# A decoder trunk on one core: the four convolution taps that TensorE took in three channel tiles go to VectorE

## The chip, the cores and the metric

One Trainium2 chip, one of its cores. The metric is device microseconds of one execution of the whole program, the median of several runs. TensorE is written PE, VectorE DVE, ScalarE ACT, GpSimd POOL and SyncE SP, as the profile writes them.

## The reference

Two layers over a sequence of 1024 positions and 1024 channels: forgetting attention and a gated convolutional feed-forward, then a Conformer convolution module and another feed-forward. The change lies in the Conformer module alone:

```
def conformer_conv(h, w_pw1, b_pw1, w_dw, b_dw, ln_g, w_pw2, b_pw2):
    u = h @ w_pw1 + b_pw1
    a, g = jnp.split(u, 2, axis=-1)
    u = a * jax.nn.sigmoid(g)
    u = causal_dwconv(u, w_dw) + b_dw
    u = rms_norm(u, ln_g)
    u = jax.nn.silu(u)
    return u @ w_pw2 + b_pw2
```

`causal_dwconv` is depthwise: each channel is convolved along the sequence with its own 31 taps (CONV_WIDTH = 31).

## The kernel before, in words

Channels lie on the 128 partitions and positions on the free axis. The sequence is taken in two halves of 512 positions; `conv(h)` (L1109) does half h, in eight channel tiles `ct` of 128 channels. fp32 products are made of three matmuls of split operands (`mm3`, L351, lines L354 to L356: high by high, low by high, high by low). A **piece** of such a product is 12 matmuls of 128x512; the weights of a piece are loaded (SP's queue), split into `whi` by ACT (L348, or L100 where the low part was stored earlier) and `wlo` by POOL or DVE (L349).

For each channel tile the module runs: four pieces of the pointwise product into two PSUM banks (`pw` in the trace); the gate (L1140), which is ACT's sigmoid `sg`, ACT's copy of 30 carried-over columns, and DVE's `u`, L1145; the taps (`taps_of`, L1169); and L1203, DVE's sum `y` of two accumulators. Of the 31 taps ten are made by ACT with POOL: ACT multiplies a shifted window (`prod`, L1195, the first one L1185) and POOL adds it to `pacc` (L1196). The others are DVE's: one instruction each, on the PSUM accumulator `cacc` (the first L1189, the next ones L1191). In the second half (`h == 1`) and the channel tiles of PE_TILES = (4, 5, 6) PE makes four of these (PE_TAPS): `on_pe` (L1159), put behind the gate, has ACT build four 128x128 diagonal matrices `dg` (L1166) and PE multiply them with the windows of `u` into `cacc` (L1167). DVE then adds its 17 taps to what PE left there.

The order of the instructions on the engines is written by hand: generators yield pieces, and `Trunk.trace` runs them with a look-ahead of a few splits. Each engine works its list in order. In the taps of a tile, `first` (L1219) mixes in other work: it counts DVE's tap instructions (`vector` of a piece) and lets a PE piece in for every BEAT = 3.6 of them, by turns from the next tile's `pw` pieces and from a `fill` generator. In the second half the fill is first the rest of the convolution's output product and its norm (transposes `nps`, L210, of the normed blocks `hn`, L201, turned into `hthi` and `htlo`, L322 and L323), then `early` (L509), the feed-forward's up-product pieces, `e` in the trace. Of these there is a fixed number in all: those not done in the taps are done later, two in the stretch in which `combine` (L447) has DVE form the factors `bhi`, `blo` of a Strassen-like product (L465 to L486), beside its first pieces `y` and `z`.

After the last tile the conv's norm follows: POOL adds the last square to `sqa` (L1217), PE sums it (`ssps`, L1253), POOL turns it into `r` (L171, L172), DVE makes a diagonal of it (L1261), PE spreads it (`rb`, L1265), DVE scales (L1271), ACT applies SiLU and casts (L1272, L1273), and the output product `dn` begins.

Of the kernel before, what the change touches and what calls it, by code (L numbers as in the profile page):

```python
# [9 lines left out]
F32 = mybir.dt.float32  # L10
F32R = mybir.dt.float32r
BF16 = mybir.dt.bfloat16
AF = mybir.ActivationFunctionType
# [4 lines left out]
P = 128  # L18
# [31 lines left out]

N_POOL = 10
ROW_BUFS = 8
PE_TAPS = 4
PE_TILES = (4, 5, 6)
GATES = (2, 1)
BEAT = (3.3, 3.6)
LAG = 3
# [57 lines left out]
class Trunk:  # L115
# [993 lines left out]
    def conv(self, xs, xd, h, ht, w_pw1, los, taps, vec, w_pw2, halo, after):  # L1109


        nc = self.nc
        C = taps.shape[1]
        H = C - 1
        n_pool = N_POOL
        wv = w_pw1.rearrange("(k p) n -> p k n", p=P)
        st = {}
        us = {}
        ys = {}
        accs = {}  # L1120

        def glu(ct):
            pss = [None, None]

            def piece(s, q):
                c0 = s * D + ct * P
                w = Weight(self, wv[:, 4 * q : 4 * q + 4, c0 : c0 + P], [P, 4, P], los[2 * ct + s][q])

                def run():
                    if q == 0:  # L1130
                        pss[s] = self.bank("pw1")
                    lh, ll = w.parts
                    hhi, hlo = ht[h]
                    for j in range(4):
                        k = 4 * q + j
                        self.mm3(pss[s], lh[:, j, :], ll[:, j, :], hhi.at(k), hlo.at(k), k == 0, k == KT - 1)

                return Piece(run, w.load, w.split, 1, tiles=1)

            def gate():  # L1140
                sg = self.part("sg")
                nc.scalar.activation(sg, pss[1], AF.Sigmoid, bias=vec[:, 1, ct : ct + 1])
                u = self.up_.tile([P, H + 512], F32, tag="u", name=self.n("u"), bufs=2)
                nc.scalar.copy(u[:, 0:H], halo[:, ct, :])
                nc.vector.scalar_tensor_tensor(  # L1145
                    u[:, H:], pss[0], vec[:, 0, ct : ct + 1], sg, op0=ALU.add, op1=ALU.mult
                )
                if h == 0:
                    nc.scalar.copy(halo[:, ct, :], u[:, 512:])
                us[ct] = u  # L1150

            for s in range(2):
                for q in range(2):
                    yield piece(s, q)
            yield Piece(gate, vector=1)
            if h == 1 and ct in PE_TILES:
                yield Piece(lambda: on_pe(ct))

        def on_pe(ct):  # L1159

            dg = self.part("dg")
            acc = accs[ct] = self.pst.tile([P, 512], F32, tag="t", name=self.n("cacc"))
            for i in range(PE_TAPS):
                j = n_pool + i
                d = dg[:, i * P : (i + 1) * P]
                nc.scalar.activation(d, self.ident, AF.Copy, scale=taps[:, j, ct : ct + 1])  # L1166
                nc.tensor.matmul(acc, d, us[ct][:, j : j + 512], start=i == 0, stop=i == PE_TAPS - 1)  # L1167

        def taps_of(ct):  # L1169
            begun = h == 1 and ct in PE_TILES  # L1170
            own = n_pool + (PE_TAPS if begun else 0)
            nv = C - own
            t = {}
            tap = lambda j: taps[:, j, ct : ct + 1]

            def some(i0, i1):
                if i0 == 0:
                    t["u"] = us.pop(ct)
                    t["acc"] = accs.pop(ct) if begun else self.pst.tile([P, 512], F32, tag="t", name=self.n("cacc"))
                    t["pacc"] = self.part("pacc")  # L1180
                    t["done"] = 0
                u, acc, pacc = t["u"], t["acc"], t["pacc"]
                win = lambda j: u[:, j : j + 512]
                if i0 == 0:
                    nc.scalar.activation(pacc, win(0), AF.Identity, bias=vec[:, 2, ct : ct + 1], scale=tap(0))  # L1185
                for i in range(i0, i1):
                    j = own + i
                    if i == 0 and not begun:
                        nc.vector.tensor_scalar(acc, win(j), tap(j), None, op0=ALU.mult)  # L1189
                    else:  # L1190
                        nc.vector.scalar_tensor_tensor(acc, win(j), tap(j), acc, op0=ALU.mult, op1=ALU.add)  # L1191
                    while t["done"] < min(n_pool - 1, (n_pool - 1) * (i + 1) // (nv - 2)):
                        t["done"] += 1
                        p = self.part("prod")
                        nc.scalar.activation(p, win(t["done"]), AF.Copy, scale=tap(t["done"]))  # L1195
                        nc.gpsimd.tensor_tensor(pacc, pacc, p, op=ALU.add)  # L1196

            def end():
                if ct == 0:
                    st["yq"] = [self.quarter("y", F32, late=True) for _ in range(2)]  # L1200
                    st["sqa"] = self.part("sqa")
                y = ys[ct] = st["yq"][ct // 4][:, ct % 4, :]
                nc.vector.tensor_tensor(y, t["acc"], t["pacc"], op=ALU.add)  # L1203

            for i in range(0, nv, 3):
                yield Piece(lambda i=i: some(i, min(i + 3, nv)), vector=min(3, nv - i))
                if i == 6 and ct > 0:
                    yield Piece(lambda: square(ct - 1))
            yield Piece(end, vector=1)

        def square(ct):
            if ct == 0:
                nc.scalar.activation(st["sqa"], ys[ct], AF.Square)
            else:
                sq = self.part("sq")
                nc.scalar.activation(sq, ys[ct], AF.Square)
                nc.gpsimd.tensor_tensor(st["sqa"], st["sqa"], sq, op=ALU.add)  # L1217

        def first(fill):  # L1219

            beat = turn = 0
            yield from glu(0)
            for ct in range(KT):
                gates = glu(ct + 1) if ct + 1 < KT else iter(())
                for t in taps_of(ct):
                    while beat > 0:

                        own = turn < GATES[h]
                        p = None
                        for g in ([gates] + fill)[:: 1 if own else -1]:  # L1230
                            if not p:
                                p = next(g, None)
                                own = g is gates
                        if not p:
                            beat = 0
                            break
                        turn = (turn + 1) % (GATES[h] + 1) if p.tiles else GATES[h] if own else 0
                        yield p
                        beat += p.vector - (BEAT[h] if p.tiles else 0)
                    yield t  # L1240
                    beat += t.vector
                for p in gates:
                    turn = GATES[h]
                    yield p
            yield Piece(lambda: square(KT - 1))
# [68 lines left out]
def trunk(ctx, tc, a):  # L1314
# [205 lines left out]
    def pieces():  # L1520
# [10 lines left out]
        down1 = ffn_down(0, 1, xds[0], conv_norm, dnlo, actlo)  # L1531
        yield from turned(down1)
        main0, norm0, rest0 = conv(0)
        yield from main0([down1])
        yield from some(down1, 3)
# [5 lines left out]
        yield from down1  # L1541
        yield from turned(rest0)
        main1, norm1, rest1 = conv(1)
        fill = [rest0]
        main1 = main1(fill)
# [59 lines left out]
```

## Time and profile before

| | |
|---|---|
| median of 3 runs | 2355.17 us (2353.74 to 2355.51) |
| the profiled execution, own time | 2358.65 us |
| its span | 2356.9 us |
| PE busy | 2270.7 us, 96% of the span |
| DVE busy | 1648.0 us, 70% |
| ACT busy | 1359.7 us, 58% |
| POOL busy | 1402.2 us, 59% |

The span runs from the first to the last instruction; the 1.75 us between it and the execution's own time lie around it. Busy time of PE comes from modelled ends of pipelined matmuls: a matmul is listed with 0.39 us, yet the next one starts 0.23 us behind it, so lengths of PE work are read from starts. The stretch that the change touches runs from about 1538 us (the gate of tile 3 in the second half) to about 1697 us (the first `dn` of the output product).

### The profile page before, as it was taken

The numbers are of one execution on the slowest core, as the hardware profiler recorded it, in microseconds if no ns is written. First come the engines' busy times: TensorE is split into PE (matmuls) and PEld (weight loads), VectorE is DVE, ScalarE is ACT, GpSimd is POOL, SyncE is SP. The second block draws the span as 40 slices with busy tenths as digits, with TensorE's granted clock in tenths as the row PEclk, the third lists the DMA queues.
The fourth block names the chain that finished last, engine by engine and source line by source line (L and its number), as shares of the span: only waits on it lengthen the run. The fifth ranks groups of instructions, "written<-read, shape, count | busy, mean of one in ns | idle before, by whom it ended". The sixth has DMA issues, their size and how long they took to land.

```text
span 2356.9 us, 35332 instructions
## 1 busy us (share of the span) xinstructions
PE 2270.7 (96%) x11306; PEld 1934.8 (82%) x11306; DVE 1648.0 (70%) x2740; ACT 1359.7 (58%) x2844; POOL 1402.2 (59%) x1187
## 2 busy tenths in 40 slices
PE   7899999999999999999999999978999999999998
PEld 7899999997878887778778887856787888888887
DVE  5577777777378999997337985885738999993222
ACT  5566666666255666666455665555635666664443
POOL 3445545444018988884454895765634999965543
PEclk9999999998999999999999999999999999999999
DMA  4222322143155556666888777533555545466664
GB/s 144 64 79 79 81 77 77 57 166 131 69 176 184 155 161 213 200 198 200 285 273 291 235 251 264 176 110 112 183 180 170 155 152 156 153 220 208 216 206 155
DMA packets 366842, 392.64 MB, mean 167 GB/s; under 512 B 26416, under 2 KB 245312, under 8 KB 366656
## 3 DMA queue, kind: packets, MB, share of 16 engines
q1 hardware_dynamic: 366656, 390.38, 52.1%
q8 instruction: 89, 1.46, 0.2%
q14 instruction: 97, 0.79, 0.1%
HBM read 299.78 MB, written 82.12 MB: 162 GB/s over the span
## 4 chain that ended last, share of the span: by engine, by line
PE 44%; DVE 18%; issue 5%; ACT 3%; DMA 2%; POOL 2%; SPq 0%; DVEq 0%; ACTq 0%; POOLq 0%
DVE acc L580 9%; PE dn L355 7%; PE dn L356 7%; PE dn L354 7%; PE pw L354 2%; PE pw L356 2%; PE pw L355 2%; DVE cacc L1191 2%; PE e L356 1%; PE e L354 1%; PE e L355 1%; ACT acc L584 1%; PE y L354 1%; PE y L355 1%; PE y L356 1%
## 5 line engine op out<-in xcount | busy, mean ns | idle before, releaser
L349 POOL TENSOR_TENSOR wlo<-raw,whi 128x512 fp32r<-128x512 f32 (+1 forms) x305 | 443.0, 1454 | 270.1 <-ACT whi L348 237.2
L348 ACT CAST whi<-raw 128x512 fp32r<-128x512 f32 (+2 forms) x497 | 302.7, 633 | 248.3 <-PE dn L355 159.2
L349 DVE TENSOR_TENSOR wlo<-raw,whi 128x512 fp32r<-128x512 f32 (+1 forms) x192 | 149.5, 783 | 236.8 <-ACT whi L348 221.3
L349 POOL TENSOR_TENSOR wlo<-s,whi 128x512 fp32r<-128x512 f32 x176 | 258.7, 1480 | 66.8 <-ACT whi L348 66.6
L354 PE MATMUL dn<-whi,whi 128*128 128x512 f32 x704 | 276.1, 392 | 1.8 <-ACT whi L348 1.3
L355 PE MATMUL dn<-wlo,whi 128*128 128x512 f32 x704 | 275.2, 391 | 0.9 <-POOL wlo L349 0.9
L356 PE MATMUL dn<-whi,wlo 128*128 128x512 f32 x704 | 275.3, 391 | 0.0
L1191 DVE SCALAR_TENSOR_TENSOR cacc<-u,ctaps,cacc 128x512 f32<-128x512 f32 x311 | 235.0, 756 | 21.9 <-PE cacc L1167 11.5
L1196 POOL TENSOR_TENSOR pacc<-pacc,prod 128x512 f32<-128x512 f32 x144 | 190.1, 1320 | 87.2 <-ACT prod L1195 80.7
L354 PE MATMUL y<-bhi,whi 128*128 128x512 f32 x528 | 207.2, 392 | 6.6 <-DVE u L638 5.2
L356 PE MATMUL y<-bhi,wlo 128*128 128x512 f32 x528 | 205.6, 389 | 0.0
L355 PE MATMUL y<-blo,whi 128*128 128x512 f32 x528 | 205.5, 389 | 0.0
L171 POOL TENSOR_SCALAR ss<-ss 128x4 f32<-128x4 f32 (+1 forms) x96 | 22.8, 238 | 298.5 <-ACT hn L191 156.3
L354 PE MATMUL pj<-whi,hthi 128*128 128x384 f32 (+1 forms) x512 | 178.1, 349 | 5.3 <-DVE zf L824 3.6
L356 PE MATMUL pj<-whi,htlo 128*128 128x384 f32 (+1 forms) x512 | 177.5, 347 | 0.0
L355 PE MATMUL pj<-wlo,hthi 128*128 128x384 f32 (+1 forms) x512 | 176.5, 345 | 0.7 <-DVE wlo L349 0.7
L914 POOL TENSOR_SCALAR x<-x,nm 128x896 f32<-128x896 f32 (+7 forms) x128 | 101.0, 794 | 107.0 <-DVE nm L913 75.3
L558 POOL TENSOR_TENSOR s<-raw,raw 128x512 f32<-128x512 f32 x88 | 124.6, 1416 | 63.7 <-DMA raw<-in_ffn_w_up_dram 35.7
L354 PEld LDWEIGHTS dn<-whi,whi 128*128 128x128 f32 x704 | 132.9, 189 | 30.3 <-ACT whi L348 1.7
L355 PEld LDWEIGHTS dn<-wlo,whi 128*128 128x128 f32 x704 | 132.9, 189 | 29.1 <-POOL wlo L349 1.2
L356 PEld LDWEIGHTS dn<-whi,wlo 128*128 128x128 f32 x704 | 132.9, 189 | 27.6
L584 ACT ACTIVATE acc<-acc 128x512 f32<-128x512 f32 x88 | 55.7, 633 | 166.2 <-DVE acc L580 164.9
(224 smaller groups left out, 6442.8 us busy)
## 6 DMA issues: line engine op xcount, KB each, us to landing
raw<-in_ffn_w_up_dram SPq DMA_DIRECT2D x240, 256.0 KB
raw<-in_ffn_w_down_dram SPq DMA_DIRECT2D x176, 256.0 KB
raw<-actd SPq DMA_DIRECT2D x152, 256.0 KB
raw<-in_conv_w_pw_dram SPq DMA_DIRECT2D x96, 256.0 KB
actd<-acc SPq DMA_DIRECT2D x76, 256.0 KB
wlo<-pwlo SPq DMA_DIRECT2D x64, 256.0 KB
raw<-in_fox_w_in_dram SPq DMA_DIRECT2D x64, 192.0 KB
xd<-x SPq DMA_DIRECT2D x24, 512.0 KB
```

What stands on the lines that cost most here:

```text
L171: nc.gpsimd.tensor_scalar(ss, ss, 1.0 / n, EPS, op0=ALU.mult, op1=ALU.add)
L348: self.nc.scalar.copy(hi, raw)
L349: (self.nc.vector if vector else self.nc.gpsimd).tensor_tensor(lo, raw, f32(hi), op=ALU.subtract)
L354: nc.tensor.matmul(out, lh, rh, start=start, stop=False, skip_group_check=more)
L355: nc.tensor.matmul(out, lh, rl, start=False, stop=False, skip_group_check=more)
L356: nc.tensor.matmul(out, ll, rh, start=False, stop=stop, skip_group_check=more)
L558: nc.gpsimd.tensor_tensor(st[o], *(st[m].rearrange("p a b -> p (a b)") if m[0] == "a" else st[m] for m in ((y, x) if o == "s4" else (x, y) ...
L580: nc.vector.scalar_tensor_tensor(acc[:, j:], ps[:, : 512 - j], tap[2 - j], acc[:, j:], op0=ALU.mult, op1=ALU.add)
L584: nc.scalar.activation(acc, acc, AF.Silu)
L914: nc.gpsimd.tensor_scalar(X[:, :L], X[:, :L], nm[:, 2:3], 1.0, op0=ALU.mult, op1=ALU.mult)
L1191: nc.vector.scalar_tensor_tensor(acc, win(j), tap(j), acc, op0=ALU.mult, op1=ALU.add)
L1196: nc.gpsimd.tensor_tensor(pacc, pacc, p, op=ALU.add)
```

## The change

PE_TAPS, PE_TILES, `on_pe` and the branches on `begun` go. Every tile of both halves has 21 taps on DVE (one L1189, twenty L1191) and ten on ACT with POOL.

```
-PE_TAPS = 4
-PE_TILES = (4, 5, 6)
...
             yield Piece(gate, vector=1)
-            if h == 1 and ct in PE_TILES:
-                yield Piece(lambda: on_pe(ct))
-
-        def on_pe(ct):
-
-            dg = self.part("dg")
-            acc = accs[ct] = self.pst.tile([P, 512], F32, tag="t", name=self.n("cacc"))
-            for i in range(PE_TAPS):
-                j = n_pool + i
-                d = dg[:, i * P : (i + 1) * P]
-                nc.scalar.activation(d, self.ident, AF.Copy, scale=taps[:, j, ct : ct + 1])
-                nc.tensor.matmul(acc, d, us[ct][:, j : j + 512], start=i == 0, stop=i == PE_TAPS - 1)
 
         def taps_of(ct):
-            begun = h == 1 and ct in PE_TILES
-            own = n_pool + (PE_TAPS if begun else 0)
-            nv = C - own
+            nv = C - n_pool
...
-                    t["acc"] = accs.pop(ct) if begun else self.pst.tile([P, 512], F32, tag="t", name=self.n("cacc"))
+                    t["acc"] = self.pst.tile([P, 512], F32, tag="t", name=self.n("cacc"))
...
                 for i in range(i0, i1):
-                    j = own + i
-                    if i == 0 and not begun:
+                    j = n_pool + i
+                    if i == 0:
                         nc.vector.tensor_scalar(acc, win(j), tap(j), None, op0=ALU.mult)
                     else:
                         nc.vector.scalar_tensor_tensor(acc, win(j), tap(j), acc, op0=ALU.mult, op1=ALU.add)
```

Up to the gate of tile 4 in the second half, each engine's list stays as it was. From there it moves, because the taps that `first` counts are more. Line numbers below are each kernel's own: L1191, L201, L210, L323, L349, L354 of before are L1174, L199, L208, L321, L347, L352 now.

PE, behind the last `pw` piece of tile 4; `cacc` is the taps' accumulator, `nps` the transposes of the normed blocks, `pw` the products of tile 5. Before:

```order
L356 MATMUL pw_3619_17569<-hthi_3415_16562,wlo_17433 128x512
L1167 MATMUL cacc_17635<-u_17631,dg_17634 128x512 x4
L210 MATMUL nps_17644<-ident,hn_17556 128x128 x4
L210 MATMUL nps_17651<-ident,hn_17556 128x128 x4
L210 MATMUL nps_17673<-ident,hn_17625 128x128 x4
L210 MATMUL nps_17680<-ident,hn_17625 128x128 x4
L354 MATMUL pw_3643_17694<-hthi_3414_16561,whi_17456 128x512
```

With the change:

```order
L354 MATMUL pw_3619_17569<-hthi_3415_16562,wlo_17433 128x512
L208 MATMUL nps_17640<-ident,hn_17556 128x128 x4
L208 MATMUL nps_17647<-ident,hn_17556 128x128 x4
L352 MATMUL pw_3638_17663<-hthi_3414_16561,whi_17456 128x512
L353 MATMUL pw_3638_17663<-htlo_3416_16563,whi_17456 128x512
```

The tap products ahead of the transposes are gone, and a `pw` piece now stands between the first and the second block's transposes. Further on, the third and the fourth block's transposes stand side by side, where a `pw` piece lay between them.

DVE at the same place, from the gate of tile 4 (`u_17631`) to its sixth tap or so; `cacc_17486` is tile 3's accumulator. Before:

```order
L1145 SCALAR_TENSOR_TENSOR u_17631<-pw_3605_17503,cvec,sg_17629 128x512
L323 TENSOR_TENSOR htlo_3603_17498<-nps_17644,hthi_3601_17496 128x4x128
L323 TENSOR_TENSOR htlo_3604_17499<-nps_17651,hthi_3602_17497 128x4x128
L201 SCALAR_TENSOR_TENSOR hn_17625<-x_16629,ss_17624,rows_16833 128x512
L201 SCALAR_TENSOR_TENSOR hn_17625<-x_16629,ss_17624,rows_16835 128x512
L1191 SCALAR_TENSOR_TENSOR cacc_17486<-u_17483,ctaps,cacc_17486 128x512 x3
L1203 TENSOR_TENSOR y_17085<-cacc_17486,pacc_17487 128x512
```

With the change:

```order
L1142 SCALAR_TENSOR_TENSOR u_17631<-pw_3605_17503,cvec,sg_17629 128x512
L1174 SCALAR_TENSOR_TENSOR cacc_17486<-u_17483,ctaps,cacc_17486 128x512 x3
L321 TENSOR_TENSOR htlo_3603_17498<-nps_17640,hthi_3601_17496 128x4x128
L321 TENSOR_TENSOR htlo_3604_17499<-nps_17647,hthi_3602_17497 128x4x128
L199 SCALAR_TENSOR_TENSOR hn_17625<-x_16629,ss_17624,rows_16833 128x512
L199 SCALAR_TENSOR_TENSOR hn_17625<-x_16629,ss_17624,rows_16835 128x512
L1186 TENSOR_TENSOR y_17085<-cacc_17486,pacc_17487 128x512
```

Tile 3's last three taps moved ahead of the `htlo` that waits for PE's transposes.

DVE in the stretch of `combine`, where the last factor `blo` is made; `wlo` is the split of an `e` piece's weight, `t` and `blo` the factors. Before:

```order
L476 TENSOR_TENSOR t_3996_19376<-t_3996_19376,htlo_3604_17499 128x512
L349 TENSOR_TENSOR wlo_19574<-raw_19361,whi_19573 128x512
L486 TENSOR_TENSOR blo_19554<-t_3980_19335,bhi_19553 128x512
L475 TENSOR_TENSOR t_4003_19412<-hthi_3602_17497,t_4003_19412 128x512
L476 TENSOR_TENSOR t_4003_19412<-t_4003_19412,htlo_3604_17499 128x512
L349 TENSOR_TENSOR wlo_19598<-raw_19401,whi_19597 128x512
L628 TENSOR_TENSOR u_4040_19614<-y_19601,p_3827_18577 128x512
```

With the change:

```order
L474 TENSOR_TENSOR t_4001_19402<-t_4001_19402,htlo_3604_17499 128x512
L484 TENSOR_TENSOR blo_19578<-t_3986_19363,bhi_19577 128x512
L473 TENSOR_TENSOR t_4007_19436<-hthi_3602_17497,t_4007_19436 128x512
L474 TENSOR_TENSOR t_4007_19436<-t_4007_19436,htlo_3604_17499 128x512
L626 TENSOR_TENSOR u_4051_19654<-y_19641,p_3833_18605 128x512
```

Two weight splits have gone from here: on PE, the two `e` pieces that stood among the first `y` and `z` pieces are done earlier. Of them one comes ahead of `ssps` and one between `rb` and the first `dn`.

## Rows read from the trace of the kernel before

**Rows 1.** The page's part 1: busy time and share of each engine.

```profile
PE 2270.7 (96%) x11306; PEld 1934.8 (82%) x11306; DVE 1648.0 (70%) x2740; ACT 1359.7 (58%) x2844; POOL 1402.2 (59%) x1187
```

**Rows 2.** Busy time by stretch: start:end, length, then each engine, PEclk, DMA.

```profile
1538.00:1558.00 20.00, 11.69 (x51) 8.98 (x49) 18.32 (x27) 13.16 (x26) 15.68 (x15) 0.95 0.24 73
1558.00:1600.00 42.00, 27.92 (x105) 18.47 (x106) 30.36 (x39) 19.11 (x36) 18.83 (x17) 0.87 0.31 110
1650.00:1674.00 24.00, 24.00 (x107) 19.88 (x107) 23.47 (x32) 14.43 (x25) 17.01 (x12) 1.00 0.56 176
```

**Rows 3.** Who waited for whom on PE, 1550 to 1698 us: total, times, longest.

```profile
PE cacc L1167 <- DVE u L1145: 16.5, 3, 8.2
PE nps L210 <- DVE hn L201: 7.6, 5, 2.2
```

**Rows 4.** PE's timeline: start, length, instruction, idle time before it and releaser.

```profile
1550.14 0.39 PE L356 MATMUL pw<-hthi,wlo 128*128 128x512 f32 x1
1558.77 5.61 PE L1167 MATMUL cacc<-u,dg 128*128 128x512 f32 x8 [8.24 <-DVE u L1145]
1564.22 1.03 PE L210 MATMUL nps<-ident,hn 128*128 128x128 f32 x8
...
1596.08 5.73 PE L1167 MATMUL cacc<-u,dg 128*128 128x512 f32 x8 [5.71 <-DVE u L1145]
...
1623.51 5.37 PE L1167 MATMUL cacc<-u,dg 128*128 128x512 f32 x8 [2.60 <-DVE u L1145]
...
1689.55 1.02 PE L1265 MATMUL rb<-dg,ones 128*128 128x512 f32 x2
1697.14 0.50 PE L354 MATMUL dn<-whi,hthi 128*128 128x512 f32 x1 [1.11 <-ACT hthi L1273]
```

**Rows 5.** Who waited for whom on DVE, 1558 to 1674.2 us.

```profile
DVE cacc L1191 <- PE cacc L1167: 11.5, 2, 5.9
DVE htlo L323 <- ACT hthi L322: 6.8, 1, 6.8
DVE wlo L349 <- ACT whi L348: 5.7, 2, 3.4
DVE y L1203 <- POOL pacc L1196: 5.4, 2, 3.9
```

**Rows 6.** DVE's timeline: a run of 16 taps, hn and gate of tile 4, y of tiles 4 and 7.

```profile
1524.86 12.63 DVE L1191 SCALAR_TENSOR_TENSOR cacc<-u,ctaps,cacc 128x512 f32<-128x512 f32 x16
1556.54 1.43 DVE L201 SCALAR_TENSOR_TENSOR hn<-x,ss,rows 128x512 f32<-128x512 f32 x2
1557.88 0.74 DVE L1145 SCALAR_TENSOR_TENSOR u<-pw,cvec,sg 128x512 f32<-128x512 f32 x1
1594.59 0.69 DVE L1203 TENSOR_TENSOR y<-cacc,pacc 128x512 f32<-128x512 f32 x1
1673.45 0.69 DVE L1203 TENSOR_TENSOR y<-cacc,pacc 128x512 f32<-128x512 f32 x1
```

**Rows 7.** PE's granted clock (behind the busy times) in pieces of 2 us.

```profile
1556.00:1558.00 2.00, 0.00 (x0) 0.00 (x0) 2.00 (x4) 0.00 (x0) 1.83 (x3) 0.50 0.62 198
1564.00:1566.00 2.00, 1.25 (x9) 0.79 (x7) 0.53 (x1) 1.15 (x3) 0.00 (x0) 1.00 0.00 0
```

**Rows 8.** The norm's chain behind the last tile: POOL's and DVE's timelines.

```profile
1674.88 1.29 POOL L1217 TENSOR_TENSOR sqa<-sqa,sq 128x512 f32<-128x512 f32 x1 [5.88 <-ACT sq L1216]
1687.23 1.89 DVE L1261 TENSOR_SCALAR dg<-ident,r 128x128 f32<-128x128 f32 x4 [5.11 <-POOL r L172]
```

**Rows 9.** The stretch of combine: PE's first and seventh piece, DVE's last blo.

```profile
1800.35 0.39 PE L354 MATMUL y<-bhi,whi 128*128 128x512 f32 x1
...
1816.67 0.39 PE L354 MATMUL y<-bhi,whi 128*128 128x512 f32 x1
...
1815.48 0.84 DVE L486 TENSOR_TENSOR blo<-t,bhi 128x512 fp32r<-128x512 f32 x1
```

**Rows 10.** The page's part 5: POOL's adds of ACT's taps, mean of one.

```profile
L1196 POOL TENSOR_TENSOR pacc<-pacc,prod 128x512 f32<-128x512 f32 x144 | 190.1, 1320 | 87.2 <-ACT prod L1195 80.7
```

More of the change, by code (lines that the diff above doesn't have):

```diff
@@ L1119, in conv @@
         ys = {}
-        accs = {}
         def glu(ct):
```

## The prediction

> **What bounds the kernel now.** Read first the busy times: PE has work for 96% of the span and DVE for 70% [rows 1], so over the whole program time is PE's, and a change shows only where PE stands still or works less. Then the stretches: from 1538 to 1600 us that picture is turned round, PE is busy in 11.69 of 20 us and in 27.92 of 42, while DVE has 18.32 of 20 and 30.36 of 42 [rows 2]. This is the stretch in which the taps run. The waits say why it is loose on both sides. PE waits 16.5 us in front of its tap products for DVE's `u`, three times, and 7.6 us in front of transposes for `hn` [rows 3]. DVE in turn waits 11.5 us for those tap products, and 6.8 us for `hthi` [rows 5], whose transposes stand right behind the first tap product on PE: that product begins at 1558.77 and the transposes at 1564.22 [rows 4]. So once per tile 4, 5 and 6, the two engines stop for one another: PE can't begin the taps before the gate's `u`, and DVE can't go on before PE has ended them. The tap products are slow as well: PE's granted clock is 0.50 of its 2.4 GHz in 1556 to 1558 and back at 1.00 only in 1564 to 1566 [rows 7], so the first tap product runs wholly at 1.2 GHz or on its way back.
>
> **The change, on DVE.** Each of the three tiles gets four more taps (17 become one L1189 and twenty L1191): 12 more in all. A tap follows the last one by 12.63 / 16 = 0.79 us [rows 6], so 9.5 us more work. From the end of tile 4's gate (1557.88 + 0.74 = 1558.6) to the end of tile 7's `y` (1673.45 + 0.69 = 1674.1) [rows 6] there are 115.5 us. DVE waits 11.5 + 6.8 + 5.7 + 5.4 = 29.4 us in them [rows 5], so it works 86.1 us; with the new taps 95.6 us. If no wait is left, `y` of tile 7 comes 19.9 us earlier. The 11.5 go with the tap products. The 6.8 go because the transposes are no longer behind them and three taps of tile 3 now stand between. The 5.7 for `whi` and the 5.4 for POOL's `pacc` stand late because ACT sat behind an `e` piece that sat behind the tap products. POOL's own work for a tile is nine adds of 1.32 us [rows 10], and a square of 1.29 us [rows 8]; with two weight splits taken at that same length it is 15.8 us, below DVE's 21 x 0.79 + gate 0.74 + `y` 0.69 = 18.0 us per tile, so POOL keeps up. I leave 2 us of waits: 17.9 us earlier. Bounds: 19.9 if none is left, 8.8 if all 11.1 us of waits on `whi` and `pacc` stay.
>
> ACT loses the twelve diagonals, which nobody waits for once the products are gone; SP's list is the same up to a few swapped neighbours. Both go at nothing: ACT is busy 19.11 of 42 us there [rows 2].
>
> **The change, on PE.** From the end of the last `pw` in front of the stall (1550.14 and the 0.23 us to where a next one would start, 1550.4) to the first `dn` at 1697.14 there are 146.8 us. Taken off it: idle 16.5 + 7.6 [rows 3] + 1.1 [rows 4] = 25.2 us, and the three tap products. These are listed with 5.61, 5.73 and 5.37 us; the first one's follower starts 5.45 us behind it [rows 4], so about 16 us together. The rest, 105.6 us, stays. Two `e` pieces come in: seven pieces' starts, 1800.35 to 1816.67, are six pieces apart, 2.72 us each [rows 9], so 5.4 us and 111.0 us of work.
>
> New idle time: the first transposes still wait for DVE's `hn`, done at 1556.54 + 1.43 = 1558.0 [rows 6]: 7.6 us. The second block's wait is covered by the `pw` piece that moved in front of it, but the third's and fourth's now have none between: DVE does three taps, a split, `htlo` and `hn` between them, some 6 us. I take the old 7.6 us again for all of these. That gap sends the clock down as the one before it did [rows 7]; the first gap's slow work ends in a wait anyway, the second one's slows the `pw` pieces of tile 5, for which I take half of four microseconds, 2 us. In front of `rb` I take 2.5 us (next paragraph). Together 19.7, so `dn` begins at 1550.4 + 130.7 = 1681.1, **16.1 us earlier**.
>
> DVE must bear that out. POOL's last square ended at 1674.88 + 1.29 = 1676.2 and `rb` began at 1689.55 [rows 8, 4], 13.4 us for the chain through `ssps`, `r` and `dg`; 17.9 us earlier it is 1658.3, and `rb` at 1671.7 if the chain is as long, some 4 us earlier if part of it was `ssps` standing behind `e` pieces. From `rb` to `dn` were 7.6 us [rows 4]; now three `e` pieces, 8.2 us, and `rb`'s own 1.0 stand there: 9.2. That gives 1677 to 1681. PE has three pieces, 8.2 us, between `ssps` and `rb`, so it comes up some 2.5 us short: that is the wait I put in. PE's sum is the later one, and decides.
>
> In the stretch of `combine` the two `e` pieces are missing: **5.4 us less**, provided that nothing they covered comes out. The first piece on the last factor began one piece behind 1816.67, at 1819.4, and would now begin at 1814.0; its last quarter, 2.0 us on, needs the last `blo`, which ended at 1815.48 + 0.84 = 1816.3 [rows 9]. Two weight splits leave DVE in front of it; at the 0.84 us of `blo` that is 1814.6 against 1816.0. It just fits.
>
> Sum: 16.1 + 5.4 = 21.5 us off the profiled execution's 2358.65, so 2337.2. The median of the runs, 2355.17, lies 3.5 us below that execution; the same 21.5 off it is **2333.7 us**. With DVE's bounds, `dn` comes 7.0 to 20.6 us earlier, and the time is 2342.8 to 2329.2.
>
> A rule that speaks against the change: in the stretch 1558 to 1600 the busiest engine is DVE, not PE [rows 2], and it is given 9.5 us more. The Trainium skill, Perfetto Trace Analysis, section Identifying the Most-Contended Engine, says that the engine with the highest occupancy is the one to relieve first. By that rule DVE's stretch would grow by the whole 9.5 us. The rows of waits decide for me: an engine that waits 29.4 us has room for 9.5. The case in which it has none is the rival "no change" below.
>
> **The rivals.** What a measurement of this kernel can tell from no change is about 0.2%, 4.7 us.
>
> *More than that.* PE runs through: of its idle time only the first 7.6 us stay, and it gains 16 + 25.2 - 7.6 = 33.6 us, time 2321.6. For it: from 1650 to 1674 PE is never idle [rows 2]. Against it: there DVE is busy 23.47 of 24 us, so DVE would have to lose more than it can (19.9).
>
> *Less.* The moved pieces were cover: without them PE waits for `blo` and the weights of `y` in `combine` and loses the 5.4 us again, and the norm's chain in front of `rb` costs 5 us more. 21.5 - 10.4 = 11.1, time 2344.1. For it: the margin at `blo` is 1.4 us.
>
> *No change.* DVE's waits keep their length under other names (`pacc`, `whi`), so the tiles grow by the 9.5 us, less the 5.4 us of the moved pieces: 2359.3. It decides where POOL's chain takes as long as a tile did, (1673.45 - 1594.59) / 3 = 26.3 us [rows 6], against my 15.8.
>
> *Slower.* PE's clock: the products that bridged part of the gaps are gone, and bursts of `pw` and `e` between the longer gaps run at 1.2 GHz. A piece costs 2.72 us more at 0.50; from eight such pieces on the 21.5 us are eaten, and at ten the time is 2355.2 + 27.2 - 21.5 = 2360.9. Against it: before, the clock was back some 5 to 7 us behind the restart [rows 7, 4], about two pieces per gap, and I see two gaps that long. The Trainium skill, TensorE: Matmul & The Clock Gate, section HAM oscillation, tells of a kernel in which every burst starts at half clock behind every gap; the row bears out the drop, not that it would repeat.
>
> That the change does not do what it says can be left out: the engines' lists show the products gone and the taps there.
>
> **How the numbers follow.** Forecast 0.70, more 0.08, less 0.11, no change 0.06, slower 0.05. The forecast's own range is 2329 to 2343; going down to 2323, towards "more", and up to 2345, over "less", leaves out the last two and part of "more". Faster by over 0.2%: 0.70 + 0.08 + 0.11 = 0.89; within 0.06; slower 0.05.
>
> **What would show it.** In the new profile: no L1167; 320 taps of the later form (311 before) and 16 first ones (13); DVE with few waits from 1558 us, and its last `y` ending near 1656; POOL's `pacc` not among DVE's long waits; `dn` beginning near 1681, PE idle some 20 us in front of it; no wait of a `y` or `z` piece in the stretch of `combine`. I am wrong if `y` of tile 7 ends later than 1665 (waits stayed), if the granted clock is below 1.00 for more than the two gaps, or if PE waits in `combine`.

## The result, and the profile with the change

| | median, us | runs | ratio to before, 95% interval |
|---|---|---|---|
| before, beside the change | 2355.28 | 4 (2353.74 to 2355.51) | |
| with the change | 2339.14 | 4 (2335.43 to 2341.47) | 0.9931 [0.9914, 0.9949] |
| with the change, once more in a later job | 2338.32 | 4 (2334.36 to 2339.73) | 0.9920 [0.9906, 0.9935] |

The change makes the kernel faster by 16.1 us in the first comparison and by 18.6 us in the second (before: 2356.93 us there). The forecast was 21.5 us less, 2333.7 us; the range of 2323 to 2345 holds both medians. The profiled execution took 2338.83 us, its span 2337.1.

The page's parts 1 and 5 of the changed kernel, and the first taps from the view of lines; they answer to [rows 1]:

```profile
PE 2259.7 (97%) x11282; PEld 1930.9 (83%) x11282; DVE 1653.6 (71%) x2751; ACT 1354.6 (58%) x2832; POOL 1405.7 (60%) x1188
...
L1174 DVE SCALAR_TENSOR_TENSOR cacc<-u,ctaps,cacc 128x512 f32<-128x512 f32 x320 | 241.7, 755 | 10.8
...
L1172 DVE TENSOR_SCALAR cacc<-u,ctaps 128x512 f32<-128x512 f32 x16 | 12.0, 749 | 0.8
```

PE lost its 24 tap matmuls; DVE has 320 later taps and 16 first ones, as the lists say. The stretches that were loose in [rows 2], in the same order of columns (start:end, length, PE, PEld, DVE, ACT, POOL, clock, DMA):

```profile
1538.00:1558.00 20.00, 13.17 (x55) 10.81 (x54) 19.39 (x28) 13.20 (x25) 17.37 (x17) 0.86 0.35 118
1558.00:1600.00 42.00, 37.11 (x159) 29.96 (x159) 39.03 (x53) 25.79 (x47) 26.76 (x23) 0.91 0.46 146
...
1650.00:1674.00 24.00, 20.00 (x80) 15.51 (x79) 11.07 (x17) 8.86 (x17) 11.78 (x10) 0.88 0.61 198
```

From 1558 to 1600 both engines are now nearly full, where they stood at 27.92 and 30.36 us of 42. The last row covers later work than it did [rows 2]: the norm's chain, which before began at 1674.88 us [rows 8], now lies in it. It shows new trouble: PE has 4 us of idle time there and a clock of 0.88. Who waited, on PE from 1548 to 1685 us, answering to [rows 3]:

```profile
PE nps L208 <- DVE hn L199: 11.7, 4, 6.8
PE rb L1248 <- DVE dg L1244: 4.0, 1, 4.0
```

and on DVE from 1556 to 1651.8 us, the end of the last `y`, answering to [rows 5]:

```profile
DVE u L1142 <- ACT sg L1139: 0.9, 1, 0.9
DVE wlo L347 <- ACT whi L346: 0.8, 1, 0.8
DVE htlo L321 <- ACT hthi L320: 0.2, 1, 0.2
```

DVE's 29.4 us of waits have become 1.9, the 2 us that the forecast left, and `pacc` is not among them. Another 2.6 us of waits for `whi` lie behind the last `y`; the expectations below count them in (4.6 us).

**A point to measure from.** The two traces differ before the place that the change touches. DVE's gate of tile 3 stands in both kernels behind the same list of instructions, and yet it starts 3.16 us sooner with the change. DVE's timeline, before:

```profile
1539.30 0.75 DVE L1145 SCALAR_TENSOR_TENSOR u<-pw,cvec,sg 128x512 f32<-128x512 f32 x1 [1.00 <-ACT sg L1142]
```

and with the change, with the last `y`:

```profile
1536.14 0.75 DVE L1142 SCALAR_TENSOR_TENSOR u<-pw,cvec,sg 128x512 f32<-128x512 f32 x1 [1.00 <-ACT sg L1139]
...
1651.04 0.68 DVE L1186 TENSOR_TENSOR y<-cacc,pacc 128x512 f32<-128x512 f32 x1
```

One variant that was profiled twice (four pieces and filled gaps, below) has this gate at 1538.88 and at 1532.97 us, but 796.8 and 796.5 us from the gate to the end of the span. So all places below are counted from this gate, the third gate of the expectations:

| us behind the gate of tile 3 | end of last `y` | `rb` begins | first `dn` | end of span |
|---|---|---|---|---|
| before | 134.8 | 150.3 | 157.8 | 817.6 |
| with the change | 115.6 | 132.8 | 144.9 | 801.0 |
| with the change, once more | 115.2 | 132.4 | 144.3 | 800.5 |
| tap products in tile 4 alone | 119.2 | 135.2 | 144.5 | 805.1 |
| tap products in tiles 5 and 6 alone | 125.9 | 140.8 | 148.6 | 806.3 |
| before, products in a bank of their own | 138.0 | 153.1 | 160.8 | 820.5 |
| before, five pieces ahead of `rb` | 134.5 | 155.3 | 162.9 | 817.6 |
| change, five pieces | 114.7 | 133.2 | 142.2 | 796.7 |
| change, four pieces | 115.7 | 132.9 | 140.6 | 796.9 |
| change, gaps filled | 115.3 | 131.3 | 140.6 | 804.4 |
| change, gaps filled, five pieces | 115.3 | 132.8 | 140.3 | 800.5 |
| change, gaps filled, four pieces | 115.3 | 130.1 | 139.1 | 796.8 |
| the same, once more | 115.0 | 129.7 | 138.8 | 796.5 |
| change, 12 taps left out | 113.9 | 130.9 | 141.7 | 795.9 |

By this the change gives 16.6 us (817.6 to 801.0), as the medians do. The last `y` is 19.3 us earlier, `rb` 17.5, the first `dn` only 13.0. PE's timeline shows where that went:

```profile
1655.62 0.95 PE L1236 MATMUL ssps<-ones,sqa 128*128 128x1 f32 x8
...
1668.89 2.07 PE L1248 MATMUL rb<-dg,ones 128*128 128x512 f32 x2 [4.00 <-DVE dg L1244]
1669.98 1.42 PE L352 MATMUL e<-hthi,whi 128*128 128x512 f32 x1
1671.19 0.63 PE L353 MATMUL e<-htlo,whi 128*128 128x512 f32 x1
...
1675.54 0.39 PE L352 MATMUL e<-hthi,whi 128*128 128x512 f32 x1
...
1680.99 0.39 PE L352 MATMUL dn<-whi,hthi 128*128 128x512 f32 x1
...
1800.98 0.39 PE L352 MATMUL z<-bhi,whi 128*128 128x512 f32 x1
```

Behind the 4.00 us of waiting, the first `e` piece lasts from 1669.98 to 1675.54, 5.56 us instead of 2.72 [rows 9]. PE's granted clock in pieces of 2 us says why (busy time of PE, clock, DMA):

```profile
1668.00:1670.00 2.00, 1.11 (x3) 0.57 0.91 348
1670.00:1672.00 2.00, 2.00 (x5) 0.50 0.06 23
1672.00:1674.00 2.00, 2.00 (x6) 0.50 0.00 0
1674.00:1676.00 2.00, 2.00 (x7) 0.72 0.00 0
1676.00:1678.00 2.00, 2.00 (x10) 1.00 0.00 0
```

It is the 1.2 GHz level for nearly 7 us. Part of why `rb` waited shows in POOL's timeline:

```profile
1652.47 1.29 POOL L1200 TENSOR_TENSOR sqa<-sqa,sq 128x512 f32<-128x512 f32 x1 [5.41 <-ACT sq L1199]
1657.56 1.73 POOL L556 TENSOR_TENSOR s<-raw,raw 128x512 f32<-128x512 f32 x1 [3.80 <-DMA c11d<-ev]
...
1664.62 0.19 POOL L169 TENSOR_SCALAR r<-r 128x4 f32<-128x4 f32 x1
1664.89 1.02 POOL L170 TENSOR_TENSOR r<-r,mhalf 128x4 f32<-128x4 f32 x1
```

The root `r` stands in POOL's list behind four sums `s` of another product's weights and a split, and the first of the sums waits 3.80 us for a transfer. Before, the sums stood in the same place but ran on 0.65 us behind the last square:

```profile
1676.82 1.30 POOL L558 TENSOR_TENSOR s<-raw,raw 128x512 f32<-128x512 f32 x1 [0.65 <-DVE wlo L349]
```

The transfer hangs on the last `y`. DVE's and SP's timelines with the change, and what SP waited for from 1653 to 1655 us:

```profile
1653.42 1.70 DVE L347 TENSOR_TENSOR wlo<-raw,whi 128x512 fp32r<-128x512 f32 x2 [1.69 <-ACT whi L346]
...
1654.34 0.37 SPq L371 DMA_DIRECT2D raw<-in_ffn_w_up_dram  x1
1654.76 0.50 SPq L232 DMA_DIRECT2D c11d<-ev  x1
...
SPq L371 <- DVE wlo L347: 2.7, 1, 2.7
```

ACT's `whi` comes behind its square of the last `y`, DVE's split `wlo` behind that `whi`, and SP's next weight load `raw` behind the first of the two splits in that row; the store named in POOL's row stands right behind this load. Before, the split in front of that load stood ahead of the last `y`: SP issued the load at 1673.56 us, and the last `y` ended at 1674.14.

### The profile page after: what moved, and what is told of

Same layout as the page of the kernel before. It is cut to its first block, busy times and chain, and to the rows that moved or that the text cites. A ratio compares the mean times of both kernels' runs of the same rounds, so it can differ in the third digit from the quotient of the medians.

```text
span 2337.1 us, 35283 instructions
## 1 busy us (share of the span) xinstructions
PE 2259.7 (97%) x11282; PEld 1930.9 (83%) x11282; DVE 1653.6 (71%) x2751; ACT 1354.6 (58%) x2832; POOL 1405.7 (60%) x1188
## 4 chain that ended last, share of the span: by engine, by line
PE 42%; DVE 19%; issue 5%; ACT 3%; DMA 3%; POOL 1%; SPq 0%; DVEq 0%; ACTq 0%; POOLq 0%
DVE acc L578 9%; PE dn L353 7%; PE dn L352 7%; PE dn L354 7%; PE pw L354 2%; PE pw L352 2%; PE pw L353 2%; DVE cacc L1174 2%; ACT acc L582 1%; PE e L352 1%; PE y L352 1%; PE e L354 1%; PE e L353 1%; PE y L353 1%; PE y L354 1%
## 5 line engine op out<-in xcount | busy, mean ns | idle before, releaser
L347 POOL TENSOR_TENSOR wlo<-raw,whi 128x512 fp32r<-128x512 f32 (+1 forms) x306 | 444.1, 1454 | 271.7 <-ACT whi L346 238.7
L347 DVE TENSOR_TENSOR wlo<-raw,whi 128x512 fp32r<-128x512 f32 (+1 forms) x191 | 144.8, 761 | 233.9 <-ACT whi L346 219.2
L347 POOL TENSOR_TENSOR wlo<-s,whi 128x512 fp32r<-128x512 f32 x176 | 258.5, 1479 | 65.1 <-ACT whi L346 64.8
L352 PE MATMUL dn<-whi,whi 128*128 128x512 f32 x704 | 276.2, 392 | 1.6 <-ACT whi L346 1.2
L354 PE MATMUL dn<-whi,wlo 128*128 128x512 f32 x704 | 275.4, 391 | 0.0
L1174 DVE SCALAR_TENSOR_TENSOR cacc<-u,ctaps,cacc 128x512 f32<-128x512 f32 x320 | 241.7, 755 | 10.8
L352 PE MATMUL y<-bhi,whi 128*128 128x512 f32 x528 | 207.7, 393 | 7.4 <-DVE u L636 5.0
L354 PE MATMUL y<-bhi,wlo 128*128 128x512 f32 x528 | 205.8, 390 | 0.0
L352 PE MATMUL pj<-whi,hthi 128*128 128x384 f32 (+1 forms) x512 | 178.0, 348 | 5.7 <-ACT v L819 2.3
L354 PE MATMUL pj<-whi,htlo 128*128 128x384 f32 (+1 forms) x512 | 177.6, 347 | 0.0
L352 PEld LDWEIGHTS dn<-whi,whi 128*128 128x128 f32 x704 | 132.9, 189 | 30.2 <-ACT whi L346 1.7
L353 PEld LDWEIGHTS dn<-wlo,whi 128*128 128x128 f32 x704 | 133.0, 189 | 29.4 <-POOL wlo L347 1.2
L354 PEld LDWEIGHTS dn<-whi,wlo 128*128 128x128 f32 x704 | 132.9, 189 | 27.8
```

Of the source, the lines that this page charges most:

```text
L347: (self.nc.vector if vector else self.nc.gpsimd).tensor_tensor(lo, raw, f32(hi), op=ALU.subtract)
L352: nc.tensor.matmul(out, lh, rh, start=start, stop=False, skip_group_check=more)
L353: nc.tensor.matmul(out, lh, rl, start=False, stop=False, skip_group_check=more)
L354: nc.tensor.matmul(out, ll, rh, start=False, stop=stop, skip_group_check=more)
```

## The experiments

**What made the loose stretch: tap products in one part of the tiles.** Two kernels, the one before with a shorter table:

```
-PE_TILES = (4, 5, 6)
+PE_TILES = (4,)
```

> TensorE keeps its taps in tile 4 alone; tiles 5 and 6 have 21 taps on VectorE. Theory A (the price is the two engines stopping for one another, wherever TensorE has taps behind a gate): tiles 5 and 6 carried 11.5 us of VectorE's waits and 8.3 us of TensorE's, so two thirds of the 16.1 us come back, ratio to before 0.9954 (about 2344.5 us); L1167 keeps 4 instructions and its first wait of about 8 us. Theory B (it was tile 4, where the transposes stand behind the tap products): little comes back, ratio 0.998 or more (2350 us and above).

```
-PE_TILES = (4, 5, 6)
+PE_TILES = (5, 6)
```

> TensorE keeps its taps in tiles 5 and 6; tile 4 has 21 taps on VectorE. Theory A: one third of the 16.1 us comes back, ratio 0.9977 (about 2350 us), and VectorE still waits about 11.5 us for the tap products in two waits. Theory B: most of it comes back, ratio 0.995 or less (2343 us and below), with the 6.8 us wait on the first hthi gone.

Measured: 2342.78 us, ratio 0.9944 [0.9931, 0.9957], with tile 4's products alone; 2346.63 us, 0.9959 [0.9947, 0.9971], with those of tiles 5 and 6. The waits of PE with tile 4's products, 1535 to 1712 us:

```profile
PE cacc L1167 <- DVE u L1145: 8.3, 1, 8.3
PE nps L210 <- DVE hn L201: 7.6, 5, 2.2
PE rb L1265 <- DVE dg L1261: 4.5, 1, 4.5
```

Freeing tiles 5 and 6 alone brings the last `y` 15.6 us forward (134.8 to 119.2), freeing tile 4 alone 8.9 us (to 125.9). Together that would be 24.5; the whole change gives 19.3. So the gains aren't additive: something else limits the last `y` from about 115 us on. By the medians the two parts give 13.5 and 9.6 us, each more than the share that theory A had for it (10.7 and 5.4), and theory B, that it was tile 4, fails with the first kernel. The other finding is the last row: with only two tiles freed, `rb` already waits 4.5 us. The wait comes with an earlier last `y` (119.2 us here), and not with one tile.

**Is it DVE's wait for PE's product itself?** Before, with the products in a bank of their own, so that DVE begins its 17 taps without them and adds the bank to `y` at the end:

```
-            acc = accs[ct] = self.pst.tile([P, 512], F32, tag="t", name=self.n("cacc"))
+            acc = accs[ct] = self.bank("pcc")
...
-                    if i == 0 and not begun:
+                    if i == 0:
...
+                if begun:
+                    nc.vector.tensor_tensor(y, y, accs.pop(ct), op=ALU.add)
```

> TensorE does its four taps in tiles 4 to 6 as before, but into a bank of its own; VectorE begins its 17 taps without them and adds them once at the end of a tile. So VectorE no longer waits for the products, while TensorE still waits for u and still does them. Theory A1 (what cost was VectorE's waiting): its 11.5 us fall to below 2, and the last y comes 7 to 9 us earlier (three more adds cost 2.1); ratio 0.996 to 0.998. Theory A2 (what cost was TensorE's own time, 16 us of products and the waits in front of them): the last y may move, the time does not, ratio 0.998 to 1.001.

Measured: 2358.82 us, 1.0012 [1.0001, 1.0023], the last `y` 3.1 us later. DVE's waits, 1556 to 1682 us:

```profile
DVE wlo L349 <- ACT whi L348: 18.6, 3, 8.9
DVE htlo L323 <- ACT hthi L322: 7.7, 1, 7.7
DVE y L1203 <- POOL pacc L1196: 5.4, 2, 4.0
```

The 11.5 us of DVE's waiting for the products [rows 5] are gone, and `wlo` waits 18.6 us where it had 5.7; the wait for `pacc` is as long as it was. PE still waited 18.0 us in front of its products for `u`, and had no new wait for the bank. The time is close to theory A2's range and far from A1's: what costs is not that DVE reads PE's sum, but what PE's list has there, the stop for `u` and the products themselves, about 16 us, with the `e` pieces, ACT's `whi` and DVE's `wlo` behind them. No run takes the stop and the products apart. For `whi` this bears out the forecast, that its wait goes along with the products.

**Do DVE's 12 new taps cost 9.5 us?** The changed kernel, with four of DVE's taps left out in each of tiles 4, 5 and 6:

```
-                    else:
+                    elif h == 0 or ct not in (4, 5, 6) or i > 4:
```

> The changed kernel with four of VectorE's taps left out in each of the tiles 4, 5 and 6 of the second half (12 taps of the convolution are not computed), the order otherwise as in the changed kernel: VectorE's load is as before the change, TensorE's taps are gone. Theory (VectorE's own list now sets the last y, at 0.79 us a tap): the last y 8 to 9.5 us earlier than the changed kernel's 115.6 us behind the third gate. If only that held the stretch, the time falls by as much (ratio 0.989 to 0.990); if TensorE's gaps and the norm's chain hold it next, the last y comes early and the first dn by no more than 4 us (ratio 0.991 to 0.993). Rival (the 12 taps filled VectorE's waits and cost nothing): last y within 2 us, ratio as the changed kernel's 0.993.

Measured: 2335.80 us, 0.9914 [0.9899, 0.9929]. The last `y` is only 1.7 us earlier (113.9 against 115.6), nearer to the rival. DVE's waits up to it, 1556 to 1652.4 us:

```profile
DVE wlo L347 <- ACT whi L346: 4.5, 4, 2.0
DVE u L1142 <- ACT sg L1139: 3.0, 2, 2.3
DVE y L1186 <- POOL pacc L1179: 0.7, 1, 0.7
DVE htlo L321 <- ACT hthi L320: 0.2, 1, 0.2
```

They are 8.4 us in all against 1.9: 6.5 us of the work left out come back as waiting. PE is busy as long as with the change: in 90.95 of the 96.3 us from 1556 us to the last `y`, there in 90.81 of 95.7. So I take it that PE's list, which reaches ACT's `whi` and `sg` through its pieces, would have set the last `y` only some 2 us sooner; that it is PE's list is read from the waits and not tested by itself. Two lists end almost together here.

The taps cost more further on: the first `dn` is 3.2 us earlier and the end 5.1 (801.0 to 795.9). The wait in front of `rb` is 2.66 us instead of 4.00, and the clock is below 1.00 for a shorter time behind it:

```profile
1668.00:1670.00 2.00, 0.72 (x3) 0.95 0.95 362
1670.00:1672.00 2.00, 2.00 (x6) 0.50 0.08 29
1672.00:1674.00 2.00, 2.00 (x8) 0.70 0.00 0
```

**The gaps at the transposes.** The changed kernel with more `pw` pieces spread among them:

```
-        yield from turned(main1, 2)
+        yield from turned(main1, 4)
```

> The changed kernel with four instead of two pieces of the gate's product spread between the transposes of tile 4 on, so that TensorE has work where it waited 6.8, 3.9 and 0.6 us for hn. Theory B1 (these gaps hang on nothing: the last y is set by VectorE's own list, which has 4.6 us of waits left): the last y within 1.5 us of the changed kernel's (97 us behind the fourth gate), ratio to the kernel before 0.992 to 0.994. Rival B2 (TensorE's list sets the stretch: each gap filled is time won): the first dn 8 to 11 us earlier than the changed kernel's, ratio 0.988 to 0.990.

Measured: 2342.33 us, 0.9939 [0.9924, 0.9954], not distinguishable from the change. The edit did not do what it was made for; PE's waits, 1548 to 1658 us:

```profile
PE nps L208 <- DVE hn L199: 9.9, 6, 3.0
PE nps L208 <- ACT sq L1199: 4.7, 1, 4.7
```

The 6.8 us gap went, but the transposes now wait 14.6 us in all instead of 11.7. The last `y` stayed at 115.3. The first `dn` comes 4.3 us earlier, yet the end comes 3.4 us later: between the gate of tile 3 and the first `dn` stand 22 `e` pieces where the change has 26, and the four missing ones, 10.9 us at 2.72 each, are done behind. What PE would gain without any gap stays open; this kernel doesn't show it.

**The wait in front of `rb`.** In the changed kernel, two more `e` pieces between `ssps` and `rb`, with which `r` also comes to stand right behind the last square on POOL:

```
         keep1["vector"] = True
-        yield from some(first, 3)
+        yield from some(first, 5)
         yield from some(norm1, 1)
```

> The changed kernel with two more up-product pieces between ssps and rb (five for three) and none of them left behind the first y piece of the next stretch; on POOL the two steps of r now stand right behind the last square instead of behind four sums and a split. Theory C (the part of the forecast that did not come lies at rb, where TensorE waited 4.0 us and then ran at half clock): the wait goes, the granted clock stays at 1.00 from 1650 to 1690 us, the stretch from ssps to the first dn is 5 to 7 us shorter beyond the two pieces moved, and the time is about 2333 us, ratio to before 0.990 to 0.991. Theory D (the missing microseconds lie in the later feed-forward, or are a matter of the runs): the ratio stays at 0.993.

Measured: 2336.74 us, 0.9916 [0.9903, 0.9928]; `rb` no longer waits, the clock is 1.00 from 1600 to 1745 us, and the end is 4.3 us nearer (801.0 to 796.7); the ratio lies between what theories C and D had. A part comes out again in the stretch of `combine`. PE's waits from 1712 to 1830 us, where the change alone has 2.7, 0.6 and 0.3 us:

```profile
PE y L352 <- DVE u L626: 4.9, 1, 4.9
PE e L354 <- DVE wlo L347: 4.3, 2, 3.6
```

So the rival "less" has a true mechanism, the moved pieces are cover; it shows when two more are taken away.

The same edit in the kernel before:

> The kernel before with the edit of the norm's cover alone: five instead of three of the e pieces stand between the last square's sum and rb, two fewer in the combine. Theory C (the wait in front of rb is made by the change: with TensorE's taps still there, the pieces ahead of rb cover the chain of the norm already, so two more cover nothing and are missed in the combine): ratio to the kernel before 0.9990 to 1.0020, no earlier start of dn beyond the 5 us that moved work explains, a new wait of y or e in the combine of 2 to 5 us. Rival D (two pieces ahead of rb are a gain by themselves, whatever the taps): 4 us less as against the changed kernel, ratio 0.9982 or below.

Measured: 2356.93 us, 1.0003 [0.9993, 1.0012]. PE has no wait in front of `rb` there, before as after the edit, and the pieces gain nothing: the wait is a product of the change, as theory C has it. The new wait in `combine` that I expected with it did not come (2.6 us for `wlo`, as before).

One piece instead of two, with nothing moved on POOL:

```
-        yield from some(first, 3)
+        yield from some(first, 4)
```

> The changed kernel with four instead of three e pieces ahead of rb and no other edit; the root r stays behind four sums of the gather on POOL in its order. Cover theory: one piece of 2.7 us covers most of the 4.0 us wait, so rb waits 1 to 1.5 us, the clock behind it falls for less time, and the first dn comes 1 to 3 us earlier measured from the third gate. Rival (the place of r on POOL is all that matters, the pieces ahead only hide part of it): the wait shrinks by the same 2.7 but the time does not, ratio within 0.0005 of the changed kernel's in the same call.

Measured: 2335.01 us, 0.9912 [0.9895, 0.9928]. PE's timeline:

```profile
1668.93 1.12 PE L1248 MATMUL rb<-dg,ones 128*128 128x512 f32 x2 [1.31 <-DVE dg L1244]
...
1676.61 0.50 PE L352 MATMUL dn<-whi,hthi 128*128 128x512 f32 x1 [1.07 <-ACT hthi L1256]
```

and its clock:

```profile
1668.00:1670.00 2.00, 1.07 (x3) 1.00 0.79 304
1670.00:1672.00 2.00, 2.00 (x11) 1.00 0.42 109
```

`rb` begins where it did (132.9 behind the gate), the wait is 2.7 us shorter, the clock stays at 1.00, and the first `dn` comes 4.3 us earlier: the covered 2.7, the 2.8 that half clock had cost, less a new wait of 1.07 for `hthi`. That is more than the 1 to 3 us expected; the end keeps 4.1 us of it.

What holds `rb` in its place is POOL's list ahead of `r`, and the transfer is one part of it. From the landing that POOL waits for to `rb` are 11.3 us with the change (1657.56 to 1668.89), 11.4 with four pieces (1657.52 to 1668.93), 11.2 with 12 taps fewer (1658.06 to 1669.28). The landing itself follows the end of the last `y` by 5.8, 5.8 and 5.7 us in these three. With the gaps filled the first sum had no such wait, and began 2.6 us behind the last `y`:

```profile
1655.73 1.28 POOL L556 TENSOR_TENSOR s<-raw,raw 128x512 f32<-128x512 f32 x1 [0.58 <-DVE wlo L347]
...
1669.09 1.38 PE L1248 MATMUL rb<-dg,ones 128*128 128x512 f32 x2 [3.82 <-DVE dg L1244]
```

Still `rb` waited 3.82 us, and 4.5 us with tile 4's products alone. The other part is PE, which comes to `ssps` sooner: 4.3 us behind the last square before, 1.9 with the change, 0.8 with the gaps filled, 0.2 with tile 4 alone.

**Both edits, and the change once more.** The filled gaps with five pieces, the filled gaps with four, this one a second time beside the change itself:

> The changed kernel with both edits, the gaps at the transposes filled and five pieces ahead of rb. Theory (the gaps hang on nothing, the wait in front of rb does): as with five pieces alone, 0.991 to 0.993. Rival (TensorE's list sets the stretch): 0.988 or below.

> The changed kernel with the gaps filled and four pieces ahead of rb instead of five, so that the combine keeps a piece behind its first y. If the cover is worth a piece's time each, up to the 4 us of the wait and the half clock behind it, and the combine's new waits (4.9 and 4.3 us with five) come from the missing piece: wait in front of rb 1 to 2 us, first y of the combine with less wait than 4.9, ratio 0.990 to 0.992, at or below that with five. If the combine's waits come from elsewhere: 0.992 to 0.993.

> The changed kernel once more, beside the variants on the same chip: ratio 0.992 to 0.994, a wait of rb of 3.5 to 4.5 us and half clock behind it, from the third gate to the last y 115.6 us and to the first dn 144.9 us within 1 us, since the order of every engine is fixed.

> The variant with the gaps filled and four pieces ahead of rb, once more and beside the changed kernel itself: 2 to 4 us below it (ratio to the kernel before 0.0008 to 0.0017 less than the changed kernel's in this call), if the wait in front of rb and the half clock behind it are what the change lost. Rival (the gain at the first dn is given back behind the combine, as it was with the gaps alone): no difference beyond 0.0005.

Measured: 2338.77 us, 0.9923 [0.9910, 0.9937]; 2335.92 us, 0.9913 [0.9899, 0.9928]; the change 2338.32 us, 0.9920 [0.9906, 0.9935]; and 2335.76 us, 0.9913 [0.9895, 0.9931]. The change's places repeat within 0.6 us, the wait of `rb` at 4.0 us. (In the kernels with filled gaps and four or five pieces `r` stands right behind the last square on POOL, and `rb` doesn't wait.) The four-piece kernels have medians 2.6 to 3.3 us below the change in the same job, and their ends lie 4 us nearer to the gate; the ratios' intervals overlap, so the places show the gain and the times only agree with it. The filled gaps add nothing to it (796.8 and 796.5 us to the end, 796.9 without them). With five pieces they end at 800.5, no better than the change, though the first `dn` is 4.5 us earlier: two `e` pieces more, 5.4 us, stand behind it. But with four pieces as many stand there, and the end is at 796.8; where these 3.7 us go no run tells. Of the kernels that end near 796.7, which the runs don't tell apart, the change with four pieces has the shortest edit.

## Why the prediction was right, and where its size was off

**DVE's term held.** I forecast the last `y` 17.9 us earlier, with 2 us of waits left and a bound of 19.9; it is 19.3, counted from the gate, with 1.9 us of waits left. The waits on `whi` and `pacc` went with the products. The separate bank shows the reverse for `whi`: it took only DVE's direct wait away, and the wait for `whi` grew from 5.7 to 18.6 us; that for `pacc` stayed at 5.4.

**What I took for the bound was half of it.** "If no wait is left" treats DVE's list as what decides, with the 12 taps at their full 9.5 us. Leaving them out gives 1.7 us. The number came out because the other list ends, as I read that run, some 2 us ahead of DVE's and not behind it; that was not in my sum, and there it had luck. The Trainium skill, Perfetto Trace Analysis, section Identifying the Most-Contended Engine, says to optimize the engine with the highest occupancy first. DVE was that engine from 1558 to 1600 us [rows 2], it was given 9.5 us more work, and its last `y` came 19.3 us earlier; read as a bar to more work for that engine, as the prediction tried it, the rule would have misled, and the rows of waits were the better guide.

**The transposes' term was near.** Forecast: 7.6 + 7.6 us of waits and 2 us of half clock. The waits are 11.7 us; behind the second gap the clock is 0.50 from 1570 to 1576 us, which by half of it is about 3 us, and behind the first the eight transposes take 1.97 us for 1.03 [rows 4]. By this estimate 15.6 us stand against 17.2.

**The mis-sized term is the one in front of `rb`**: "PE has three pieces, 8.2 us, between `ssps` and `rb`, so it comes up some 2.5 us short: that is the wait I put in." The runs show 4.0 us of wait and, behind it, 2.8 us more for a piece at half clock, 6.8 for 2.5. I had put `rb` at 17.9 us earlier and it is 17.5; but PE reached it sooner than my sum has it, and I gave this gap no clock price though I had given the transposes' gap one. The norm's chain became longer, 15.1 us from POOL's last square (1653.76) to `rb` against 13.4, though the prediction had it as long as before: `r` stands behind sums that now wait for a transfer, and that transfer is issued behind the last `y` where it was issued ahead of its end. The first `dn` is 13.0 us earlier instead of 16.1. That its clock time in the trace is 16.15 us earlier is chance: 3.16 of it were there before the change's first instruction. One piece of cover gives 4.1 us back at the end, which is the greater part of what the forecast had too much (21.5 against 16.6).

**`combine` held.** From the first `dn` to the `z` piece at which both lists are in step again, 1822.11 us before and 1800.98 now, it takes 124.97 and 119.99 us: 5.0 us less for the forecast 5.4, with waits of 0.6 and 0.3 us for `y`. A wait of PE there was on my list of signs that I am wrong; it came, but cost under 1 us. Another 1.4 us is lost between there and the end (16.6 of 18.0); no experiment looked at it, and it stays open.

**The rivals.** "More" failed at DVE's bound and PE's gaps. "Less" named both things that can go wrong, and one did, at `rb`, with 4.3 us of its 5 (6.8 for 2.5); `combine` did so only with more pieces moved. "No change" needed `pacc` or `whi` to keep DVE waiting; up to the last `y` they had 0.8 us. "Slower" needed half clock in eight pieces; up to the first `dn` there were three gaps with it, one more than I saw, and the clock was back some 5 to 7 us behind each restart. The kernel before had three as well, one at each tap product (0.50 in 1556 to 1562, 1594 to 1600 and for most of 1624 to 1628 us); my rows showed the first alone. By my own list a third such place was a sign that I am wrong, and so it was, for one term.

**The range.** Its lower end takes `dn` 20.6 us earlier from DVE's bounds. These give 18.1 (16.1 and the 2.0 that 19.9 has over 17.9); the other 2.5 are the whole wait in front of `rb`, which the same 2.0 us would have shortened already. So by its own terms the forecast reached down to 2331.7 us, not 2329.2; the measured time lies on the other side.

## What to carry to other kernels

When a work item of an engine waits for another engine, look at what stands behind it in that engine's list: giving it a buffer of its own gained nothing here, and moving it to the engine with the waits did. Its 9.5 us of work cost 1.7 us at the last `y` there, and 5.1 at the end. A chain that is to move forward must be followed through every list that it passes: what stands ahead of its steps, for which transfer that waits, and what that transfer's issue waits for. And where a change lets an engine run dry at a new place, count the wait and the pieces at half clock behind it, and look for a piece of later work to put in front.

## Of the hardware, not expected

Behind a wait of 4.0 us in front of `rb` PE's clock went from 1.00 to 0.50 for nearly 7 us, in both executions of the change; behind one of 2.66 us (12 taps left out) and one of 3.82 us (gaps filled) it went to 0.50 for between 3 and 4 us; with 1.31 us it stayed at 1.00. So the longer wait did not always bring the longer stretch at half clock. Between four pieces and the change 2.7 us more of waiting cost 5.5 us, a half of which no row of waits shows.

One kernel, with one list of instructions, reached the gate of tile 3 at 1538.88 us in one profiled execution and at 1532.97 in another. These 5.9 us are a third of the change's whole effect, and no part of it; behind the gate the two executions agree within 0.3 us.
